# Where the operands of TensorE begin in a 64-byte line of SBUF

## The chip, the cores and the metric

One core of one Trainium2 chip (trn2). The time is the device time of one execution in microseconds (us), the median of several runs. The kernel before takes 1748.18 us, the median of three runs from 1745.37 to 1749.04.

## The reference

The input is 256 tokens of width 1024, in float32. Two blocks follow each other.

The first block is a token mixer and a layer of experts. The mixer projects the normed input to gates, a short causal convolution and an mLSTM of 8 heads; its two branches are projected, gated and added, and projected once more. The experts are PEER: 8 heads pick 16 of 16384 experts for each token, and `out = gelu(h @ u) * gate @ v` is taken over the picked ones.

The second block has two layers, one with latent attention (MLA), one with attention over q, k and v (MoBA, which at this length is plain attention with a bias by distance). Each is followed by a layer norm, a convolved and gated feed-forward network (FFN) with 22 chunks of 128 hidden columns, and a layer norm.

```
h  = modulate(rms_norm(x))           # per block and layer
y  = h @ W                           # q, k, v, gates, branches, u, v, FFN in and out
```

Nearly all work is matrix products of the 256 tokens with weights of 1024 rows or columns.

## The kernel before, in words

Activations lie transposed: 128 partitions, 8 chunks (`KC`) of the model width, 256 tokens (`T`). Weights come from HBM as slabs of 128 x 1024 float32 values, 512 KB each, into `wraw`. To keep float32 precision every operand is split into a high part (`hi`, of type float32r, made by a copy on ScalarE, ACT) and a low part (the rest, made by a subtraction on VectorE, DVE). A product is then three matmuls: high by high, high by low, low by high. `mm3` (L398 to L403) issues them: with weights as the stationary operand, loaded anew for each matmul, and the activations as the moving operand of 256 columns: whi with the activation's high part (L401), whi with its low part (L402), wlo with its high part (L403). `block` does this for the 8 chunks of a slab, 24 matmuls; `half` (L473 to L475) does the same for the output projections of the attentions.

In three projections to values (`vform`, L448 to L450: w_v, ml_uv, mo_v) and in the expert output (`row`, L1276 to L1278, 128 slabs of v) the roles are turned: the activation is stationary, and the slab's high and low parts, whi and wlo, are the moving operands, 512 columns at a time.

The order of the work is written out by hand. `use` takes the next slab of a plan, starts the load of a later one on SP's queue (5 slabs ahead) and splits the next ones (`warm`, L312 and L320, three buffers each for whi and wlo, `buffer` gives them). Small generators that evacuate PSUM and do the element-wise work are advanced before and after each block. While the chip does this, loads of the modulation matrices (`mraw`, L519) run at a rate set for each stage (`RATES`).

The pairs of activations are named after their stage: h (mixer input), ya, ym, mx (mixer), h2 (expert input), hh and hl (inputs of the second block's layers; the mixer's h bears the names hh and hl in the trace as well), o (attention output), lat (latent), gb (FFN hidden), pre (before a layer norm).

A pool gives its tiles one after the other, at multiples of 32 bytes. `off_line` (L590) asks for a tile of 32 bytes and leaves it unused, so that what follows begins half a line of 64 bytes further on. By the sizes in the code and the addresses that the compiled program gives its tiles, all pairs but two begin 32 bytes into such a line, high and low part alike: h, ya, ym, mx, h2, hh, lat, both o, and gb of layer 0. The first exception is gb of layer 1, where `4 * l` words are left out at the front (L1803): its high part begins 16 bytes in and its low part 48. The second is pre, whose rows are 258 words long, so that each chunk begins 8 bytes further on. The slabs whi and wlo begin at 0, and so do ah and al, the stationary operands of the expert output.

Of the kernel before, what the change touches and what calls it, by code (L numbers as in the profile page):

```python
# [11 lines left out]
F32 = mybir.dt.float32  # L12
F32R = mybir.dt.float32r
# [8 lines left out]
P = 128  # L22
T = 256
D = 1024
KC = 8
# [20 lines left out]
ROW_UNITS = 8  # L46
PAUSES = [3, 2, 2, 2, 2, 2, 2, 1, 0, 3, 3]
NFF = 22
EPS = 1e-6
LN_EPS = 1e-5  # L50
TINY = 1e-30
# [213 lines left out]
class Body:  # L265
# [64 lines left out]
    def buffer(self, n, pool, part, name):  # L330
        if n in self.spare:
            return self.spare[n][part]
        if self.extra and n >= self.n_extra and (n - self.n_extra) % 5 < 2:
            pool = self.extra[part]
        return pool.tile([P, D], F32R, name=name)

    def load(self, n):
        if self.plan is None:
# [248 lines left out]
        nc.gpsimd.tensor_tensor(r[:, :width], v[:, :width], self.mhalf[:, :width], ALU.pow)  # L587
        return r

    def off_line(self, pool, name):  # L590

        pool.tile([P, 8], F32, name="half" + name)

    def pool_l(self, name, bufs=1):
        return self.tc.tile_pool(name=name, bufs=bufs, reuse_waits="tile")
# [117 lines left out]
    def mixer(self):  # L713
        nc, a = self.nc, self.a
        with ExitStack() as ctx:
            self.tmps = ctx.enter_context(self.pool_l("tmps1", 14))
            sp = ctx.enter_context(self.pool_l("mix", 1))
            self.mctx = ExitStack()
            mp = self.mctx.enter_context(self.pool_r("mraw", 4))
            rp = ctx.enter_context(self.pool_l("mixr", 2))  # L720
            act8 = lambda n, tag=None: (sp.tile([P, KC, T], F32R, name=n + "h", tag=(tag or n) + "h"),
                                         sp.tile([P, KC, T], F32R, name=n + "l", tag=(tag or n) + "l"))
            f8 = lambda n, tag=None: sp.tile([P, KC, T], F32, name=n, tag=tag or n)
            x = self.x

# [4 lines left out]
            v = {}  # L730
# [12 lines left out]
            for w in LOADS:  # L743
                n = int(w[1])
# [14 lines left out]
            st = self.pst()  # L759
            xn = f8("xn", "qk")  # L760
            a1 = self.cp.tile([P, KC], F32, name="a1")
            self.off_line(sp, "h")
            h = act8("h")
            ws, lows, pts = [], {}, {}
            pair = [sp.tile([P, 2, D], F32R, name="w3" + m, tag="ya" + m) for m in "hl"]
            for n in range(3, START_SLABS):
                self.spare[n] = [t[:, n - 3] for t in pair]

# [49 lines left out]
            for w in START:  # L818
                if w in left:
                    n = left.index(w) + 1  # L820
# [144 lines left out]
            ya = act8("ya")  # L965
# [26 lines left out]
            for j in range(8):  # L992
                gc, gx, gb = g_cxb(j)
# [2 lines left out]
                self.block("w_x", j, h, gx)  # L996
                self.block("w_b", j, h, gb)

            self.off_line(sp, "ym")
            ym = act8("ym")  # L1000

            def g_fin():
# [108 lines left out]
    def peer(self):  # L1111
        tc, nc, a = self.tc, self.nc, self.a
        NB = 88
        with ExitStack() as ctx:
            self.tmps = ctx.enter_context(self.pool_l("tmps2", 4))
            sp = ctx.enter_context(self.pool_l("pe", 1))
# [2 lines left out]
            iT.append(sp.tile([P, T // 2], F32, name="nT"))  # L1119
            hctx = ExitStack()  # L1120
            hp = hctx.enter_context(self.pool_l("peh", 1))
            self.off_line(hp, "h2")
            h = (hp.tile([P, KC, T], F32R, name="h2h"), hp.tile([P, KC, T], F32R, name="h2l"))
            r = self.rstd(self.st2, 2, EPS, D)
            self.rows.step(PAUSES[9])
            bc = self.bcast2(r)
# [29 lines left out]
            zb = gp = None  # L1156
# [71 lines left out]
            for i2 in range(P):  # L1228
                if i2 == N0:
                    for _ in self.side or ():  # L1230
                        pass
                    self.side = None
                    tctx.close()
                    zp = zctx.enter_context(self.pool_r("zb", 1))
                    zb = zp.tile([P, P - NB, T], F32, name="zb")
                    self.off_line(zp, "zb")
                    gctx = ExitStack()
                    gp = gctx.enter_context(self.pool_l("oneh", 2))
                if i2 >= N0 and ng < 64:
                    self.spawn(g_group(ng))  # L1240
                    ng += 1
                if i2 == N0 + 67:
                    gctx.close()
                    vp2 = zctx.enter_context(self.pool_r("pv2", 2))
                    asplit(0)
                self.block("u", i2, h, g_z(i2))
# [41 lines left out]
            for i2 in range(P - 1):  # L1288
                w = self.use(("v", i2, 0, D))
# [21 lines left out]
            w = self.use(("v", P - 1, 0, D))  # L1311
# [5 lines left out]
            part = lambda tt, hf: yt[:, (2 * tt + hf) * 512:(2 * tt + hf + 1) * 512]  # L1317
# [35 lines left out]
            self.xctx = ExitStack()  # L1353
            xp = self.xctx.enter_context(self.pool_r("xp2"))
            x2 = xp.tile([P, KC, T], F32, name="x2")
            h = self.h = (xp.tile([P, KC, T], F32R, name="hh"), xp.tile([P, KC, T], F32R, name="hl"))
            crow = xp.tile([P, D], F32, name="crow")
            nc.sync.dma_start(crow, self.crow)
            self.crow = crow
            self.rt = xp.tile([P, 3, T], F32, name="rt")  # L1360
            nc.sync.dma_start(self.rt, rt[:, 0:3])
            ht = za[:, 16:24]
            piece = lambda j: tr[j // 2][:, (j % 2) * T:(j % 2 + 1) * T]
# [224 lines left out]
    def ln_cols(self, idx, nxt, pre=None):  # L1588
        nc = self.nc
        g, b = self.colr("ln_g", 8 * idx, 8), self.colr("ln_b", 8 * idx, 8)  # L1590
        AB = ag = None
        self.pre = pre
        if nxt is not None:
            s, c = nxt
            AB = self.cp.tile([P, KC, 2], F32, name=f"lnAB{idx}")
            for n, w in enumerate((g, b)):
                nc.vector.scalar_tensor_tensor(AB[:, :, n], c, 1.0, w, op0=ALU.add, op1=ALU.mult)
            nc.vector.tensor_tensor(AB[:, :, 1], AB[:, :, 1], s, ALU.add)
            self.split(AB, pre[0][:, :, T:], pre[1][:, :, T:])
            ag = self.cp.tile([P, 16], F32, name=f"lnag{idx}")  # L1600
            nc.vector.tensor_scalar_mul(ag[:, 0:8], g, ALPHA)
            nc.vector.tensor_scalar_mul(ag[:, 8:16], b, ALPHA)
        self.lnc = g, b, AB, ag
        self.lnb, self.lnbs = {}, (self.lnbuf[:, :T], self.lnbuf[:, T:])
# [191 lines left out]
    def ffn(self, l, act, ctx, pts, prate=0.0):  # L1796

        nc = self.nc
        sp = ctx.enter_context(self.pool_l(f"ffn{l}", 1))
        if l == 0:  # L1800
            self.off_line(sp, "gb")

        gh, gl = (sp.tile([P, NFF * T + 4 * l], F32R, name="gb" + n)[:, 4 * l:].rearrange("p (a t) -> p a t", t=T) for n in "hl")  # L1803

        def g_ab(j):
            ge = {}

            def ga(pt):
                ac = self.tmp("fa")
                taps = [self.col("fconv", (3 * l + t) * NFF + j) for t in range(3)]  # L1810
                nc.scalar.activation(ac, pt[:, :T], AF.Identity, bias=self.col("fconvb", l * NFF + j), scale=taps[2])
                yield "post"
                for t in (1, 0):
                    s = 2 - t
                    nc.vector.scalar_tensor_tensor(ac[:, s:T], pt[:, 0:T - s], taps[t], ac[:, s:T], op0=ALU.mult, op1=ALU.add)
                nc.scalar.activation(ac, ac, AF.Gelu_apprx_tanh)
                ge[0] = ac

            def gb(pt):
                if j < NFF - 1:  # L1820
                    yield "post"
                y = self.tmp("fy")
                nc.vector.tensor_tensor(y, pt[:, :T], ge[0], ALU.mult)
                nc.scalar.activation(gh[:, j], y, AF.Copy)
                yield "post"
                self.lo_of(y, gh[:, j], gl[:, j])
            return ga, gb
        gens = [g for j in range(NFF) for g in g_ab(j)]
        names = self.ffn_names(l)
        for g, pt in zip(gens, pts):  # L1830
            self.spawn(self.g_lead(g)(pt))
        self.blocks(names[3:6], act, gens[3:6])
        for k in range(6, len(names)):
            if k == 12:
                self.prate = prate
            self.block(*names[k], act, gens[k])
        return gh, gl

    def second(self):
        nc = self.nc  # L1840
        with ExitStack() as ctx:
            self.tmps = ctx.enter_context(self.pool_l("tmps3", 12))
            sp = ctx.enter_context(self.pool_l("s2", 1))
            self.mpool = ctx.enter_context(self.pool_l("mraw3", 2))
            self.prs = ctx.enter_context(self.pool_l("pairs", 3))
            act8 = lambda pool, n: (pool.tile([P, KC, T], F32R, name=n + "h"), pool.tile([P, KC, T], F32R, name=n + "l"))
            self.z = sp.tile([P, KC, T], F32, name="z")
            h = self.h
            hx = ctx.enter_context(self.pool_l("whi2", 2)), ctx.enter_context(self.pool_l("wlo2", 2))
# [24 lines left out]
            mctx = ExitStack()  # L1874
            sp = mctx.enter_context(self.pool_l("mla", 1))
            self.rp = mctx.enter_context(self.pool_l("mlar", 3))
            self.off_line(sp, "o")
            o = act8(sp, "o")
            lat = sp.tile([P, 4, T], F32, name="lat")
            la = (sp.tile([P, 4, T], F32R, name="lath"), sp.tile([P, 4, T], F32R, name="latl"))  # L1880
            sts = {}

            def g_lat(b):
# [105 lines left out]
            gb = self.ffn(0, h, fctx, pts, RATES[2])  # L1989
# [10 lines left out]
            mctx = ExitStack()  # L2000
            sp = mctx.enter_context(self.pool_l("moba", 1))
            self.rp = mctx.enter_context(self.pool_l("mobar", 3))
            self.off_line(sp, "o")
            o = act8(sp, "o")
            vs = sp.tile([P, 2, D], F32, name="vs")
            qn, kn = qk_of(sp)

# [37 lines left out]
            gb = self.ffn(1, h, fctx, pts, RATES[5])  # L2045
# [32 lines left out]
```

## Time and profile before

| | |
|---|---|
| Median of three runs | 1748.18 us |
| The profiled execution's own time | 1751.12 us |
| Its span, first to last instruction | 1749.4 us |
| PE (TensorE matmul) busy | 1716.4 us, 98% |
| DVE (VectorE) busy | 1383.5 us, 79% |
| ACT (ScalarE) busy | 1040.0 us, 59% |
| DMA engines, mean rate | 212 GB/s |
| Granted TensorE clock, mean | 0.992 |

The busy time of PE is the union of its matmuls, which overlap one another: a matmul is recorded from the start of its reading to the modelled end of its writing. How fast PE goes is seen in the distance between the starts of two neighbours, and that is had from the number of matmuls in a stretch. [...]

### The profile page before, as it was taken

The page shows a single profiled execution, that of the slowest core. Times are in us where ns is not written, and L with a number is a line of the kernel's source. Part 1 is how long each engine was busy: PE and PEld are TensorE (multiplying, and loading weights), DVE is VectorE, ACT ScalarE, POOL GpSimd, SP SyncE. Part 2 cuts the span into 40 slices and gives each one's busy share as a digit, 9 for nine tenths or more (in the row PEclk, how much of TensorE's full clock was granted, in tenths as well). Part 3 has the DMA queues.
Part 4 walks back from the last instruction along what each step waited for, and adds up shares of the span by engine and source line. Part 5 has one row for each costly group of instructions (what it writes and reads, how often), then busy time and mean ns, then how long its engine had stood idle before and what let it go on. Part 6 is the DMA issues. An engine that isn't in the chain of part 4 may idle for free.

```text
span 1749.4 us, 33343 instructions
## 1 busy us (share of the span) xinstructions
PE 1716.4 (98%) x12720; PEld 1598.1 (91%) x12720; DVE 1383.5 (79%) x2845; ACT 1040.0 (59%) x1910; POOL 198.4 (11%) x235
## 2 busy tenths in 40 slices
PE   8999999999999999999999999989999999999997
PEld 4899999799999999998888888888999998999997
DVE  3788778589988889997888888876799778688754
ACT  3764444455554999985555554555676547567542
POOL 1110000000010654540000000030200000020001
PEclk8999999999999999999999999999999999999998
DMA  7676677555555544447898888852467674446552
GB/s 271 247 263 215 229 253 242 193 170 171 192 181 181 169 157 158 157 159 251 299 326 300 288 299 306 286 199 97 129 229 277 249 250 163 149 130 207 188 180 77
DMA packets 102400, 371.17 MB, mean 212 GB/s; under 512 B 11456, under 2 KB 11968, under 8 KB 101856
## 3 DMA queue, kind: packets, MB, share of 16 engines
q1 hardware_dynamic: 101664, 365.76, 61.6%
q0 software_dynamic: 576, 3.29, 0.5%
q8 instruction: 99, 1.62, 0.4%
q14 instruction: 61, 0.50, 0.1%
HBM read 365.99 MB, written 2.10 MB: 210 GB/s over the span
## 4 chain that ended last, share of the span: by engine, by line
PE 90%; DVE 4%; ACT 3%; issue 1%; DMA 1%; POOL 1%; POOLq 0%; ACTq 0%; DVEq 0%; SPq 0%
PE ps L401 19%; PE ps L403 19%; PE ps L402 19%; PE ps L1277 6%; PE ps L1278 6%; PE ps L1276 6%; PE ps L1205 2%; PE ps L568 1%; PE ps L448 1%; PE ps L449 1%; PE ps L450 1%; PE ps L473 1%; PE ps L739 1%; PE ps L475 1%; PE ps L474 1%
## 5 line engine op out<-in xcount | busy, mean ns | idle before, releaser
L312 ACT ACTIVATE whi<-wraw 128x1024 fp32r<-128x1024 f32 (+1 forms) x548 | 574.2, 1050 | 446.9 <-PE ps L402 195.5
L320 DVE TENSOR_TENSOR wlo<-wraw,whi 128x1024 fp32r<-128x1024 f32 (+1 forms) x538 | 649.7, 1212 | 51.7 <-ACT whi L312 50.5
L401 PE MATMUL ps<-hh,whi 128*128 128x256 f32 x1240 | 352.9, 285 | 1.9 <-ACT hh L675 1.5
L403 PE MATMUL ps<-hh,wlo 128*128 128x256 f32 x1240 | 348.5, 281 | 4.5 <-DVE wlo L320 4.5
L402 PE MATMUL ps<-hl,whi 128*128 128x256 f32 x1240 | 348.1, 281 | 1.5 <-DVE hl L397 1.3
L401 PE MATMUL ps<-h2h,whi 128*128 128x256 f32 x1152 | 329.9, 286 | 0.0
L403 PE MATMUL ps<-h2h,wlo 128*128 128x256 f32 x1152 | 322.3, 280 | 0.2 <-DVE wlo L320 0.2
L402 PE MATMUL ps<-h2l,whi 128*128 128x256 f32 x1152 | 321.3, 279 | 0.0
L401 PEld LDWEIGHTS ps<-hh,whi 128*128 128x128 f32 x1240 | 234.1, 189 | 5.4 <-ACT hh L675 2.6
L403 PEld LDWEIGHTS ps<-hh,wlo 128*128 128x128 f32 x1240 | 233.9, 189 | 5.4 <-DVE wlo L320 5.4
L402 PEld LDWEIGHTS ps<-hl,whi 128*128 128x128 f32 x1240 | 234.0, 189 | 3.1 <-DVE hl L397 2.8
L403 PEld LDWEIGHTS ps<-h2h,wlo 128*128 128x128 f32 x1152 | 216.4, 188 | 0.6 <-DVE wlo L320 0.6
L401 PEld LDWEIGHTS ps<-h2h,whi 128*128 128x128 f32 x1152 | 216.5, 188 | 0.4 <-ACT za L673 0.4
L402 PEld LDWEIGHTS ps<-h2l,whi 128*128 128x128 f32 x1152 | 216.9, 188 | 0.0
L1277 PE MATMUL ps<-whi,al 128*128 128x512 f32 x512 | 199.5, 390 | 0.8 <-DVE al L397 0.8
L1278 PE MATMUL ps<-wlo,ah 128*128 128x512 f32 x512 | 199.2, 389 | 0.0
L1276 PE MATMUL ps<-whi,ah 128*128 128x512 f32 x512 | 199.2, 389 | 0.0
L519 DVE SCALAR_TENSOR_TENSOR mraw<-mraw,crow 128x1024 f32<-128x1024 f32 x128 | 157.0, 1227 | 0.0
L1197 POOL TENSOR_SCALAR L<-iota,i1T,eT 128x128 bf16<-128x128 f32 x128 | 123.2, 970 | 295.9 <-DVE mT L1498 139.1
L1277 PEld LDWEIGHTS ps<-whi,al 128*128 128x128 f32 x512 | 96.1, 188 | 22.1 <-DVE al L397 1.9
L1276 PEld LDWEIGHTS ps<-whi,ah 128*128 128x128 f32 x512 | 96.1, 188 | 19.9
L1278 PEld LDWEIGHTS ps<-wlo,ah 128*128 128x128 f32 x512 | 96.1, 188 | 19.8
(449 smaller groups left out, 2971.8 us busy)
## 6 DMA issues: line engine op xcount, KB each, us to landing
wraw<-u SPq DMA_DIRECT2D x128, 512.0 KB, 3.3
wraw<-v SPq DMA_DIRECT2D x128, 512.0 KB, 5.4
mraw<-mod SPq DMA_DIRECT2D x88, 512.0 KB, 3.9
wraw<-fa SPq DMA_DIRECT2D x44, 512.0 KB, 4.1
wraw<-fb SPq DMA_DIRECT2D x44, 512.0 KB, 4.3
mraw<-w_ada SPq DMA_DIRECT2D x40, 512.0 KB, 4.2
wraw<-fo SPq DMA_DIRECT2D x32, 512.0 KB, 4.5
wraw<-wq SPq DMA_DIRECT2D x16, 512.0 KB, 4.3
```

Source lines behind the costliest of these rows:

```text
L312: nc.scalar.activation(t[:, :hi - lo], self.raws[self.n_hi][:, :hi - lo], AF.Copy)
L320: e.tensor_tensor(t[:, :n], self.raws[self.n_lo][:, :n], self.his[self.n_lo].bitcast(F32)[:, :n], ALU.subtract)
L401: mm(out, lh, rh, start=start, stop=False, **kw)
L402: mm(out, lh, rl, start=False, stop=False, **kw)
L403: mm(out, ll, rh, start=False, stop=stop, **kw)
L448: mm(pts[tt][hf], ah, wh[:, s], start=kc == 0, stop=False)
L519: nc.vector.scalar_tensor_tensor(raw, raw, 1.0, self.crow, op0=ALU.mult, op1=ALU.mult, accum_out=acc)
L1197: nc.gpsimd.tensor_scalar(L[:, k], iota, i1, e, op0=ALU.is_equal, op1=ALU.mult)
L1205: nc.tensor.matmul(pg[:, k * P:(k + 1) * P], L[:, k], half[:, k, h], start=h == 1, stop=h == 0)
L1276: mm(o, ah, w[0][:, s], start=first, stop=False)
L1277: mm(o, al, w[0][:, s], start=False, stop=False)
L1278: mm(o, ah, w[1][:, s], start=False, stop=last)
```

## The change

A table `AT` gives each pair two places in a line, in words of 4 bytes, for the high and the low part. `acts` asks for a tile that is one line (16 words) longer than needed and takes the part of it that begins at that place. The pads of `off_line` in front of the pairs go; one pad of 32 bytes is kept or put where the tiles before or after would otherwise lie off a line (`half_line`, in front of ym, behind zb and behind rt). whi and wlo become one line longer too, and a slab that will be moving (`MOVING`: w_v, v, ml_uv, mo_v) begins 16 bytes in (whi) or 48 (wlo), unless it falls on the two extra buffers of the second block, which stay at 0; a slab that will be stationary begins at 0 as before. Two small constants of each layer norm, `lnAB` and `lnag`, move from the pool `cp` to a pool of the second block, 384 bytes in all, as much as whi and wlo gain.

The starts, in bytes into a 64-byte line, high part / low part:

| pair | before | after |
|---|---|---|
| h (mixer) | 32 / 32 | 16 / 16 |
| ya | 32 / 32 | 4 / 4 |
| ym | 32 / 32 | 60 / 60 |
| mx | 32 / 32 | 48 / 48 |
| h2 (experts) | 32 / 32 | 16 / 48 |
| hh (second block) | 32 / 32 | 16 / 48 |
| lat | 32 / 32 | 8 / 8 |
| o, first and second attention | 32 / 32 | 48 / 16 and 0 / 32 |
| gb, layer 0 | 32 / 32 | 4 / 4 |
| gb, layer 1 | 16 / 48 | 8 / 56 |
| whi / wlo as moving operands | 0 / 0 | 16 / 48 |

```diff
+LINE = 16
+AT = dict(h=(4, 4), ya=(1, 1), ym=(15, 15), mx=(12, 12), h2=(4, 12), hh=(4, 12), la=(2, 2), o0=(12, 4), o1=(0, 8), gb0=(1, 1),
+          gb1=(2, 14), w=(4, 12))
+MOVING = ("w_v", "v", "ml_uv", "mo_v")
...
         if self.extra and n >= self.n_extra and (n - self.n_extra) % 5 < 2:
-            pool = self.extra[part]
-        return pool.tile([P, D], F32R, name=name)
+            return self.extra[part].tile([P, D], F32R, name=name)
+        at = AT["w"][part] if self.plan[n][0] in MOVING else 0
+        return pool.tile([P, D + LINE], F32R, name=name)[:, at:at + D]
...
-    def off_line(self, pool, name):
-
-        pool.tile([P, 8], F32, name="half" + name)
+    def acts(self, pool, name, kc=KC, tag=None):
+
+        return tuple(pool.tile([P, kc * T + LINE], F32R, name=name + m, tag=(tag or name) + m)[:, at:at + kc * T]
+                     .rearrange("p (a t) -> p a t", t=T) for m, at in zip("hl", AT[name]))
+
+    def half_line(self, pool, name):
+
+        pool.tile([P, LINE // 2], F32, name="half" + name)
...
-            self.off_line(hp, "h2")
-            h = (hp.tile([P, KC, T], F32R, name="h2h"), hp.tile([P, KC, T], F32R, name="h2l"))
+            h = self.acts(hp, "h2")
...
-            h = self.h = (xp.tile([P, KC, T], F32R, name="hh"), xp.tile([P, KC, T], F32R, name="hl"))
+            h = self.h = self.acts(xp, "hh")
...
+            self.half_line(xp, "rt")
...
-            AB = self.cp.tile([P, KC, 2], F32, name=f"lnAB{idx}")
+            AB = self.np.tile([P, KC, 2], F32, name=f"lnAB{idx}")
...
-        gh, gl = (sp.tile([P, NFF * T + 4 * l], F32R, name="gb" + n)[:, 4 * l:].rearrange("p (a t) -> p a t", t=T) for n in "hl")
+        gh, gl = self.acts(sp, f"gb{l}", NFF)
...
```

## Rows read from the trace of the kernel before

**Rows 1.** The page: PE's busy time and instructions; the granted clock in 40 slices.
```profile
PE 1716.4 (98%) x12720; PEld 1598.1 (91%) x12720; DVE 1383.5 (79%) x2845; ACT 1040.0 (59%) x1910; POOL 198.4 (11%) x235
...
PEclk8999999999999999999999999999999999999998
```

**Rows 2.** The page: the chain that ended last, by engine and line.
```profile
PE 90%; DVE 4%; ACT 3%; issue 1%; DMA 1%; POOL 1%; POOLq 0%; ACTq 0%; DVEq 0%; SPq 0%
PE ps L401 19%; PE ps L403 19%; PE ps L402 19%; PE ps L1277 6%; PE ps L1278 6%; PE ps L1276 6%; PE ps L1205 2%; PE ps L568 1%; PE ps L448 1%; PE ps L449 1%; PE ps L450 1%; PE ps L473 1%; PE ps L739 1%; PE ps L475 1%; PE ps L474 1%
```

**Rows 3.** Stretches: A:B, length, each engine's busy time (count), clock, DMA share, GB/s.
```profile
78.50:90.00 11.50, 11.50 (x51) 9.27 (x50) 11.26 (x21) 6.09 (x10) 0.02 (x1) 1.00 0.97 367
102.00:116.00 14.00, 14.00 (x123) 14.00 (x122) 10.54 (x16) 8.25 (x14) 0.00 (x0) 1.00 0.94 348
...
398.00:488.00 90.00, 90.00 (x767) 90.00 (x766) 85.63 (x281) 47.07 (x69) 0.00 (x0) 1.00 0.57 187
500.00:558.00 58.00, 58.00 (x500) 58.00 (x499) 54.95 (x145) 30.87 (x45) 3.60 (x3) 1.00 0.58 187
830.00:1120.00 290.00, 290.00 (x1281) 239.99 (x1280) 242.66 (x410) 151.95 (x225) 1.68 (x3) 1.00 0.87 302
1300.00:1370.00 70.00, 70.00 (x597) 70.00 (x596) 65.62 (x115) 43.63 (x67) 0.00 (x0) 1.00 0.80 282
1373.60:1435.60 62.00, 62.00 (x529) 62.00 (x528) 47.38 (x75) 30.44 (x41) 0.00 (x0) 1.00 0.70 249
1600.00:1670.00 70.00, 70.00 (x602) 70.00 (x601) 51.39 (x76) 42.63 (x66) 0.00 (x0) 1.00 0.59 189
1675.90:1736.50 60.60, 60.60 (x526) 60.60 (x526) 31.08 (x42) 22.31 (x28) 0.00 (x0) 1.00 0.41 127
```

**Rows 4.** Lines 402, 474 and 1276: count, duration (min/median/max), first and last start.
```profile
L402 PE MATMUL ps<-hl,whi x1240: 276/278/416, 37.9 to 1675.6; 128*128 128x256 f32 x177, 128*40 128x256 f32 x1
L402 PE MATMUL ps<-h2l,whi x1152: 276/278/282, 342.2 to 791.1; 128*128 128x256 f32 x192
L402 PE MATMUL ps<-gbl,whi x352: 275/276/278, 1373.7 to 1736.6; 128*128 128x256 f32 x176
...
L402 PE MATMUL ps<-yal,whi x64: 277/280/282, 251.6 to 275.3; 128*128 128x256 f32 x64
L402 PE MATMUL ps<-yml,whi x64: 276/281/288, 275.6 to 298.1; 128*128 128x256 f32 x64
L402 PE MATMUL ps<-mxl,whi x64: 277/279/385, 298.5 to 321.5; 128*128 128x256 f32 x64
L402 PE MATMUL ps<-latl,whi x48: 277/280/282, 1169.0 to 1197.6; 128*128 128x256 f32 x48
...
L474 PE MATMUL ps<-ol,whi x128: 277/280/281, 1210.5 to 1541.4; 128*128 128x256 f32 x128
...
L1276 PE MATMUL ps<-whi,ah x512: 388/389/398, 791.4 to 1140.5; 128*128 128x512 f32 x171
```

**Rows 5.** Tile gbh: ScalarE's writes in the FFN of layer 0 and of layer 1.
```profile
L1824 ACT ACTIVATE gbh<-t_fy x15: 400/419/422, 1293.6 to 1368.7; 128x256 fp32r<-128x256 f32 x15
...
L1824 ACT ACTIVATE gbh<-t_fy x16: 400/400/420, 1590.2 to 1671.1; 128x256 fp32r<-128x256 f32 x16
```

**Rows 6.** Line 1205, the one-hot matmuls of the experts: count, durations, first and last start.
```profile
L1205 PE MATMUL ps<-R,L x512: 218/219/233, 570.7 to 782.8; 128*128 128x128 f16 x171
```

**Rows 7.** Waits in the expert output: who waited for whom, us, times, longest.
```profile
ACT whi L312 <- DMA wraw<-v: 4.2, 2, 2.2
...
PE ps L1277 <- DVE al L397: 0.8, 2, 0.7
```

More of the change, by code (lines that the diff above doesn't have):

```diff
@@ L720, in mixer @@
             rp = ctx.enter_context(self.pool_l("mixr", 2))
-            act8 = lambda n, tag=None: (sp.tile([P, KC, T], F32R, name=n + "h", tag=(tag or n) + "h"),
-                                         sp.tile([P, KC, T], F32R, name=n + "l", tag=(tag or n) + "l"))
+            act8 = lambda n, tag=None: self.acts(sp, n, tag=tag)
             f8 = lambda n, tag=None: sp.tile([P, KC, T], F32, name=n, tag=tag or n)
@@ L761, in mixer @@
             a1 = self.cp.tile([P, KC], F32, name="a1")
-            self.off_line(sp, "h")
             h = act8("h")
             ws, lows, pts = [], {}, {}
-            pair = [sp.tile([P, 2, D], F32R, name="w3" + m, tag="ya" + m) for m in "hl"]
+            pair = [sp.tile([P, 2 * D + LINE], F32R, name="w3" + m, tag="ya" + m)[:, :2 * D].rearrange("p (a t) -> p a t", t=D) for m in "hl"]
             for n in range(3, START_SLABS):
@@ L997, in mixer @@
                 self.block("w_b", j, h, gb)
-            self.off_line(sp, "ym")
+            self.half_line(sp, "ym")
             ym = act8("ym")
@@ L1235, in peer @@
                     zb = zp.tile([P, P - NB, T], F32, name="zb")
-                    self.off_line(zp, "zb")
+                    self.half_line(zp, "zb")
                     gctx = ExitStack()
@@ L1599, in ln_cols @@
             self.split(AB, pre[0][:, :, T:], pre[1][:, :, T:])
-            ag = self.cp.tile([P, 16], F32, name=f"lnag{idx}")
+            ag = self.np.tile([P, 16], F32, name=f"lnag{idx}")
             nc.vector.tensor_scalar_mul(ag[:, 0:8], g, ALPHA)
@@ L1799, in ffn @@
         sp = ctx.enter_context(self.pool_l(f"ffn{l}", 1))
-        if l == 0:
-            self.off_line(sp, "gb")
-        gh, gl = (sp.tile([P, NFF * T + 4 * l], F32R, name="gb" + n)[:, 4 * l:].rearrange("p (a t) -> p a t", t=T) for n in "hl")
+        gh, gl = self.acts(sp, f"gb{l}", NFF)
         def g_ab(j):
@@ L1843, in second @@
             sp = ctx.enter_context(self.pool_l("s2", 1))
+            self.np = ctx.enter_context(self.pool_l("lnc", 1))
             self.mpool = ctx.enter_context(self.pool_l("mraw3", 2))
             self.prs = ctx.enter_context(self.pool_l("pairs", 3))
-            act8 = lambda pool, n: (pool.tile([P, KC, T], F32R, name=n + "h"), pool.tile([P, KC, T], F32R, name=n + "l"))
             self.z = sp.tile([P, KC, T], F32, name="z")
@@ L1876, in second @@
             self.rp = mctx.enter_context(self.pool_l("mlar", 3))
-            self.off_line(sp, "o")
-            o = act8(sp, "o")
+            o = self.acts(sp, "o0")
             lat = sp.tile([P, 4, T], F32, name="lat")
-            la = (sp.tile([P, 4, T], F32R, name="lath"), sp.tile([P, 4, T], F32R, name="latl"))
+            la = self.acts(sp, "la", 4)
             sts = {}
@@ L2002, in second @@
             self.rp = mctx.enter_context(self.pool_l("mobar", 3))
-            self.off_line(sp, "o")
-            o = act8(sp, "o")
+            o = self.acts(sp, "o1")
             vs = sp.tile([P, 2, D], F32, name="vs")
```

## The prediction

> **What bounds the kernel now.** [...] The view to read is the table of stretches. A stretch in which PE is busy throughout and does one kind of matmul gives the distance: its length plus one duration (0.28 us for 256 columns, 0.39 for 512), divided by the count, since the count includes what overlaps its start.
>
> That gives, in ns per matmul [rows 3]:
> - 256 columns, high and low parts both 32 bytes into a line: 90.28/767 = 117.7 and 58.28/500 = 116.6 (h2), 70.28/597 = 117.7 and 70.28/602 = 116.7 (hh, the two FFN layers), 62.28/529 = 117.7 (gb, layer 0), 14.28/123 = 116.1 (h of the mixer; one matmul more or less there is 1 ns).
> - 256 columns, high part 16 bytes in and low part 48 (gb of layer 1, the one pair that has such starts already): 60.88/526 = 115.7.
> - 512 columns, moving slab at 0: 290.39/1281 = 226.7 with the stationary side at 0 too (expert output), 11.89/51 = 233.2 with the stationary side 32 bytes in (`vform`).
>
> The clock is 1.00 in all these stretches, so it explains none of the differences. The two rows of gb do the same work on the same buffers, layer for layer; only the starts differ, and layer 1 is 2.0 ns a matmul ahead of layer 0. That is the evidence for a gain. The evidence against reading it too surely is in the same table: with nothing but 32/32 the distance is 116.6 in one stretch and 117.7 in the next, in the very same loop. A part of what separates two rows is thus not the start.
>
> **The change part by part.** No instruction, transfer or wait is added or removed; the parts are the starts of the operands, pair by pair. I price a matmul at 16/48 at 115.7, and the state of today at the mean of the rows for that tile.
>
> 1. h2, 32/32 to 16/48: 1152 groups of three [rows 4] = 3456 matmuls. Today (767 x 117.7 + 500 x 116.6)/1267 = 117.3; 1.6 ns less, 3456 x 1.6 = 5.5 us. Bounds: 0.9 ns (today all at 116.6) gives 3.1, 2.0 ns gives 6.9.
> 2. hh, 32/32 to 16/48: of the 1240 groups that stand under the names hl and whi [rows 4], 440 are the mixer's h (57 blocks of 8, less 16 groups that run from a spare buffer); 800 remain, 2400 matmuls. Today the mean of 117.7 and 116.7, 1.5 ns more than 115.7: 3.6 us, bounds 2.4 and 4.8.
> 3. o of the first attention, 32/32 to 48/16: half of 128 groups, 192 matmuls [rows 4]: 0.3 us.
> 4. The value slabs, 0 to 16 (whi) and 48 (wlo), with 512 columns: 1536 matmuls in the expert output [rows 4], and some 200 in the three `vform` calls. No row shows a 512-column read from such a start. The nearest row on one side is gb's step, about 1.5 ns a matmul whatever its length: 2.3 us saved. The nearest on the other is the step between the two 512-column rows, 233.2 − 226.7 = 6.5 ns for an operand that leaves the line's start: 1536 x 6.5 = 10.0 us lost. The same step taken as a gain is the far bound of the third rival. I take 2.3 us saved, as gb's row is of the very starts that these slabs get.
> 5. h of the mixer, 32/32 to 16/16: 456 groups, 1368 matmuls. Equal starts other than 32 stand in no steady row; between nothing and 116.6 − 115.7 = 0.9 ns: I take 0.7, 1.0 us.
> 6. ya (4/4), ym (60/60), mx (48/48), lat (8/8), o of the second attention (0/32), gb layer 0 (4/4) and layer 1 (8/56): 64 x 3 + 48 + 64 + 352 = 656 groups [rows 4], 1968 matmuls, whose new starts no row shows. gb's step of 2.0 ns either way bounds them: 3.9 us won or lost. I take nothing; layer 1 gives up the best row there is, layer 0 leaves the worst.
> 7. Side effects. ScalarE's write of gb takes 400 to 419 ns at 32 and 400 at 16, so starts off 32 don't slow the writers [rows 5]; were they slower by 19 ns a piece, ACT and DVE have room in all stretches of [rows 3] (the fullest long one is DVE's in h2, 85.63 of 90 us). The one-hot tiles of line 1205 lose their 32 bytes with h2's pad: 512 matmuls [rows 6], with the 6.5 ns step 3.3 us either way; I take nothing. `lnAB` and `lnag` move to another pool and are written by the same instructions, on DVE and beside PE's matmuls: nothing.
>
> Sum: 5.5 + 3.6 + 0.3 + 2.3 + 1.0 = 12.7 us. All of it lies on PE, which sets the end. What could be late next: a slab's period in h2 falls by 1.4%, so DVE goes from 95% to 96.5% of it; in the mixer the DMA engines are at 0.94 of their time and up to 0.97 in its `vform`, so the 1.0 us of part 5 is the least sure; in the expert output the DMA engines go from 0.87 to 0.88 of their time [rows 3], and a transfer has ended ScalarE's wait there for 4.2 us in all, DVE has held PE for 0.8 [rows 7]. Neither takes back more than 1 us. The profiled execution took 1751.1 us (span 1749.4 and 1.7 around it), so it would take 1738.4; it lies 2.9 us over the median of the runs, and from that median, 1748.2, the sum gives 1735.5.
>
> [...]
>
> **The rivals.**
> - The 512-column slabs lose (slower). [...] For it: 233.2 against 226.7, for leaving the start on one side only. Against it: there it is the stationary side, and gb's step shows that places inside the line differ. Price 10.0 us: 1758. It decides where the distance in the expert output passes 226.7 and the 12.7 − 2.3 = 10.4 us of the other parts are not won either. Chance 9%.
> - The start doesn't matter, the rows show two or three rhythms into which the same stream falls. For it: 116.6 and 117.7 with the same starts. Against it: 115.7 is seen only with 16/48, over a whole layer. Then the starts at 16 and 48 change nothing, and those that are no multiple of 16 (4, 8, 56 and 60: ya, ym, lat and both gb, 64 x 2 + 48 + 352 = 528 groups, 1584 matmuls) may cost gb's 2.0 ns, 3.2 us: 1748 to 1751. Chance 13%. [...]
> - All parts reach their good end: 6.9 + 4.8 + 0.4 + 10.0 + 1.2 + 3.9 = 27.2 us, 1721; half the way there from the forecast is 1728. Chance of more than 20 us saved: 15%.
> - The change doesn't do what it says: if a pool begins 32 bytes off from what the sizes in the code give, 16/48 becomes 48/16 and 4 becomes 36. Chance 3%; the time would lie anywhere between 1735 and 1752.
>
> **How the numbers follow.** The forecast, 4 to 20 us saved (1728 to 1744), has 60%; the rest is above. Its time is 1735.5. The 80% range leaves out the upper half of the first two rivals and the far end of the third: 1722 to 1749. A change of under 0.2%, 3.5 us, can't be told from none here. Faster by that: 60 + 15 + 2 of the last rival's 3, 77%; the same: 12%, most of the second rival and the last one's third; slower: 11%, the first rival and the end of the second.
>
> **What would show it.** In the profile after: 115.7 in the stretches of h2 and hh; below 226.7 in the expert output; the same counts of instructions. Wrong steps show as 116.6 to 117.7 in h2 and hh (second rival), or as 228 and more in the expert output (first rival). A new PE wait for DVE in h2 or for a slab's transfer in the expert output would show that the gain was won and given back.

## The result, and the profile after

The changed kernel takes 1764.3 us (median of 4 runs, 1762.97 to 1765.61), the kernel before beside it 1746.78 us (4 runs, 1743.95 to 1749.04). The ratio is 1.0101, 95% interval 1.0082 to 1.0121: slower by 1%, where 1735.5 us was forecast and 1749 was the end of the range. The profiled execution took 1763.19 us with a span of 1761.4. The two medians lie 17.5 us apart, the two profiled executions 12.0: that of before was the slowest of its four runs. The traces account for the 12.0; what makes up the rest is not shown.

What the page shows is a kernel that does the same work: PE's 12720 matmuls, and the counts and busy times of DVE and ACT (1384.0 and 1040.2 us), are those of before, the times to within 0.5 us [rows 1].

```profile
PE 1728.5 (98%) x12720; PEld 1607.2 (91%) x12720; DVE 1384.0 (79%) x2845; ACT 1040.2 (59%) x1910; POOL 196.0 (11%) x235
...
PEclk9999999999999999999999999999999999999998
```

PE waits, all told, hardly longer than it did: the rows of its waits come to 23.9 us before and 24.3 after. From the page of before, then from that of after, two of the costliest groups; last on the line is the idle time just before, and what ended it (before had 0.8 us at the last of them [rows 7]):

```profile
L403 PE MATMUL ps<-h2h,wlo 128*128 128x256 f32 x1152 | 322.3, 280 | 0.2 <-DVE wlo L320 0.2
```
```profile
L409 PE MATMUL ps<-h2h,wlo 128*128 128x256 f32 x1152 | 323.7, 281 | 1.9 <-DVE wlo L325 1.9
...
L1285 PE MATMUL ps<-whi,al 128*128 128x512 f32 x512 | 202.1, 395 | 0.6 <-DVE al L403 0.5
```

One wait for wlo in h2 has grown from 0.2 to 1.9 us; it is 0.2 to 1.3 in the kernels below. But for that, the 12.0 us by which the two spans differ lie in the time from one matmul's start to the next one's. The stretches of [rows 3], in the profile after (the short ones at the front are left out: the stages lie elsewhere in time):

```profile
398.00:488.00 90.00, 90.00 (x761) 90.00 (x760) 85.52 (x281) 46.27 (x68) 0.00 (x0) 1.00 0.56 182
500.00:558.00 58.00, 58.00 (x491) 58.00 (x490) 54.53 (x143) 30.38 (x47) 5.16 (x4) 1.00 0.57 187
830.00:1120.00 290.00, 290.00 (x1259) 236.35 (x1258) 238.96 (x404) 148.95 (x220) 1.68 (x3) 1.00 0.85 297
1300.00:1370.00 70.00, 70.00 (x597) 70.00 (x596) 67.33 (x116) 45.79 (x71) 0.00 (x0) 1.00 0.83 293
...
1600.00:1670.00 70.00, 70.00 (x597) 70.00 (x596) 53.95 (x80) 45.33 (x72) 0.00 (x0) 1.00 0.63 202
```

The clock is 1.00 throughout. Counted as in the prediction, (length + one duration)/count: h2 118.6 and 118.7 ns a matmul (before 117.7 and 116.6), the expert output 230.7 (226.7), hh 117.7 and 117.7 (117.7 and 116.7). Where 115.7 was forecast, no stretch shown is below 117.7.

A second reading needs no stretch. Line 408 (402 before) issues one matmul of each group of three, and its rows give the first and the last start of a stage:

```profile
L408 PE MATMUL ps<-h2l,whi x1152: 275/281/288, 341.2 to 794.3; 128*128 128x256 f32 x192
...
L408 PE MATMUL ps<-gb0l,whi x176: 277/283/290, 1381.6 to 1445.0; 128*128 128x256 f32 x176
L408 PE MATMUL ps<-gb1l,whi x176: 280/283/288, 1685.3 to 1748.5; 128*128 128x256 f32 x176
...
L408 PE MATMUL ps<-yal,whi x64: 277/285/290, 249.9 to 274.3; 128*128 128x256 f32 x64
L408 PE MATMUL ps<-yml,whi x64: 276/278/283, 274.7 to 296.9; 128*128 128x256 f32 x64
...
L408 PE MATMUL ps<-lal,whi x48: 278/283/287, 1177.8 to 1206.9; 128*128 128x256 f32 x48
...
L1284 PE MATMUL ps<-whi,ah x512: 388/392/397, 794.5 to 1149.2; 128*128 128x512 f32 x171
```

Against [rows 4], stage by stage, in us:

| stage | before | after | differs |
|---|---|---|---|
| up to h2's first start | 342.2 | 341.2 | −1.0 |
| h2, first to last start | 448.9 | 453.1 | +4.2 |
| expert output, first to last start | 349.1 | 354.7 | +5.6 |
| from there to the end of the span | 608.9 | 612.2 | +3.3 |

With −0.1 between the second and the third this is the 12.0. The first row hides a loss: the first matmul of the mixer's h starts 3.0 us earlier in the profile after (34.9 against 37.9 us), and the stage from there to h2 takes 2.0 longer. In the last row, gb of layer 0 takes 63.4 us instead of 61.8 and gb of layer 1 63.2 instead of 60.6 (before: 175 groups of three at the 117.7 and 115.7 of [rows 3] are 61.8 and 60.7). A group of three is the best unit for what follows: (last − first)/(count − 1). For the expert output it goes from 349.1/511 = 683.2 to 354.7/511 = 694.1 ns; the 226.7 and 230.7 of the stretches, times three, are 680.1 and 692.1, without the few groups that wait.

### The profile page after: what moved, and what is told of

Read it like the earlier page. It is cut to its first block, busy times and chain, and to the rows that moved or that the text cites. A ratio compares the mean times of both kernels' runs of the same rounds, so it can differ in the third digit from the quotient of the medians.

```text
span 1761.4 us, 33342 instructions
## 1 busy us (share of the span) xinstructions
PE 1728.5 (98%) x12720; PEld 1607.2 (91%) x12720; DVE 1384.0 (79%) x2845; ACT 1040.2 (59%) x1910; POOL 196.0 (11%) x235
## 4 chain that ended last, share of the span: by engine, by line
PE 71%; DVE 4%; ACT 2%; issue 1%; POOL 0%; DMA 0%; POOLq 0%; ACTq 0%; DVEq 0%
PE ps L407 15%; PE ps L408 15%; PE ps L409 15%; PE ps L1285 6%; PE ps L1284 5%; PE ps L1286 5%; PE ps L1213 2%; DVE wlo L325 1%; PE ps L479 1%; PE ps L480 1%; PE ps L481 1%; DVE mraw L525 1%; PE ps L574 1%; PE ps L454 1%; PE ps L456 1%
## 5 line engine op out<-in xcount | busy, mean ns | idle before, releaser
L409 PE MATMUL ps<-hhh,wlo 128*128 128x256 f32 x800 | 224.4, 280 | 4.1 <-DVE wlo L325 4.1
L407 PE MATMUL ps<-hhh,whi 128*128 128x256 f32 x800 | 227.1, 284 | 0.8 <-ACT hhh L686 0.8
L408 PE MATMUL ps<-hhl,whi 128*128 128x256 f32 x800 | 225.7, 282 | 1.2 <-DVE hhl L403 1.1
L409 PEld LDWEIGHTS ps<-hhh,wlo 128*128 128x128 f32 x800 | 150.8, 188 | 4.7 <-DVE wlo L325 4.7
L408 PEld LDWEIGHTS ps<-hhl,whi 128*128 128x128 f32 x800 | 151.1, 189 | 2.7 <-DVE hhl L403 2.4
L407 PEld LDWEIGHTS ps<-hhh,whi 128*128 128x128 f32 x800 | 151.3, 189 | 2.0 <-ACT hhh L686 1.6
L407 PE MATMUL ps<-hh,whi 128*128 128x256 f32 (+1 forms) x440 | 126.0, 286 | 0.7 <-ACT hh L686 0.7
L408 PE MATMUL ps<-hl,whi 128*128 128x256 f32 (+1 forms) x440 | 123.6, 281 | 0.2 <-DVE hl L403 0.2
L409 PE MATMUL ps<-hh,wlo 128*128 128x256 f32 (+1 forms) x440 | 123.4, 280 | 0.3 <-DVE wlo L325 0.3
```

The source lines that it names most:

```text
L407: mm(out, lh, rh, start=start, stop=False, **kw)
L408: mm(out, lh, rl, start=False, stop=False, **kw)
L409: mm(out, ll, rh, start=False, stop=stop, **kw)
```

## The experiments

The places of operands below are taken from the addresses in the compiled programs. "Distance" is from here on the place of the moving operand minus that of the stationary one, modulo 256 bytes. The line of 64 bytes is only a unit for naming starts; no run shows that the memory has such lines. Two first theories stand in the first expectation, A and B; C came after its miss. Each row shown is the line that issues the second matmul of a group (for the expert output the first, `ps<-whi,ah`).

**The pairs alone.** The changed kernel with the slabs as they were before, 1024 words long and at 0:

```
-        at = AT["w"][part] if self.plan[n][0] in MOVING else 0
-        return pool.tile([P, D + LINE], F32R, name=name)[:, at:at + D]
+        return pool.tile([P, D], F32R, name=name)
```

> The pairs of activations at the new starts, the slabs whi and wlo 1024 words long and at 0 as before. Theory A (spacing of the buffers): with a line more each, the three whi and three wlo buffers lie alternately in the first and the second half of 128 bytes, and the matmuls of a group lose where whi and wlo are not in the same half. Then h2 falls from 118.4 ns a matmul (355.2 a group of three) to 116.4 (349.2), the second block's hh from 117.8 to 116.4, the expert output from 230.5 back to 226.7; total 1764.3 - 6.9 - 3.4 - 5.5 - 2 = 1746 to 1748. Theory B (the starts themselves are the cost): h2 and hh stay at 118, only the expert output comes back; 1758. Both: gb, ya and lat (starts 4 and 8) stay at 120 to 121.

Measured: 1762.28 us, ratio to before 1.0072 (1.0049 to 1.0096).

```profile
L407 PE MATMUL ps<-h2l,whi x1152: 275/281/284, 342.1 to 788.0; 128*128 128x256 f32 x192
...
L1283 PE MATMUL ps<-whi,ah x512: 390/393/404, 788.3 to 1145.7; 128*128 128x512 f32 x171
```

h2 takes 445.9 us, 3.0 less than before: the gain forecast for it is there in part. But the expert output, whose slabs and stationary tiles have their old starts in a line, is slower than in either kernel: 357.4 us, 699.4 ns a group. Neither theory had that. What is left of the change in that stage is that `lnAB` and `lnag`, 384 bytes, have left a pool that lies ahead of the slabs: whi and wlo lie 384 bytes lower, while ah and al, in a pool on the other side of the memory, stay. Theory C is that this distance decides.

**The slabs alone.** The kernel before with the slabs' part of the change and the constants' move; the pairs as before. Then the same with all slabs at 0, so that they are only a line longer:

```
+        at = AT["w"][part] if self.plan[n][0] in MOVING else 0
+        return pool.tile([P, D + LINE], F32R, name=name)[:, at:at + D]
...
-AT = dict(w=(4, 12))
+AT = dict(w=(0, 0))
```

> The kernel before with the slab part alone: whi and wlo one line longer, moving ones at 16 and 48; all pairs as before. Theory A: h2 rises from 117.5 to some 118.5 to 119, hh and the mixer too, the expert output is at 230 as in the changed kernel; 1757 to 1760. Theory B: the pairs stay at 117.1 to 117.5, only the expert output loses 5.5 us: 1752.

> The kernel before with whi and wlo one line longer, but every slab at 0: the spacing of the buffers alone. Theory A: h2 and hh rise as in the kernel with the slab part alone; the expert output loses a part of its 3.8 ns a matmul too; 1752 to 1757. Theory B: nothing changes, 1747.

Measured: 1760.11 us, ratio 1.0074 (1.0045 to 1.0102), and 1760.2 us, ratio 1.0072 (1.0047 to 1.0097). First the one, then the other:

```profile
L407 PE MATMUL ps<-h2l,whi x1152: 277/280/285, 341.6 to 793.8; 128*128 128x256 f32 x192
...
L1281 PE MATMUL ps<-whi,ah x512: 387/392/400, 794.1 to 1148.7; 128*128 128x512 f32 x171
```
```profile
L407 PE MATMUL ps<-h2l,whi x1152: 277/280/285, 341.8 to 793.2; 128*128 128x256 f32 x192
...
L1281 PE MATMUL ps<-whi,ah x512: 388/393/398, 793.4 to 1148.2; 128*128 128x512 f32 x171
```

452.2 and 451.4 us in h2, 354.6 and 354.8 in the expert output. Moving the slabs to 16 and 48 makes no difference to the stage as a whole. What both kernels share does: the slabs are 64 bytes longer, so that neighbouring buffers no longer have the same place modulo 256, and the constants have moved. Sorted by the buffer that a slab fell on, h2's groups without a wait take 353.3, 353.7 and 357.5 ns in the first kernel (352.4 before, on all three), and the expert output 690.2, 688.8 and 696.0 (680.3). In the second kernel the same three buffers take 696.0, 688.2 and 689.2 in the expert output, with whi at distances of 128, 0 and 192 instead of 144, 16 and 208. So 16 bytes more or less are worth up to 7 ns a group, either way, and cancel over the three.

**All pairs at 16/48**, slabs as before, the constants still moved:

```
...
+AT = {n: (4, 12) for n in "h ya ym mx h2 hh la o0 o1 gb0 gb1".split()}
...
-        at = AT["w"][part] if self.plan[n][0] in MOVING else 0
-        return pool.tile([P, D + LINE], F32R, name=name)[:, at:at + D]
+        return pool.tile([P, D], F32R, name=name)
```

> Slabs as before, every pair at 16 / 48 (h, ya, ym, mx, lat, both o, both gb as well as h2 and hh). Theory A: all 256-column groups near 116.4 or 115.7 a matmul; 1738 to 1741, the best of the four, and against the kernel with the new starts and the old slabs gb, ya and lat gain 5 ns a matmul, 6 us in all. Theory B: all 256-column groups at 118; 1755.

Measured: 1758.52 us, ratio 1.0063 (1.0038 to 1.0088).

```profile
L406 PE MATMUL ps<-gb0l,whi x176: 279/286/286, 1374.8 to 1437.3; 128*128 128x256 f32 x176
L406 PE MATMUL ps<-gb1l,whi x176: 279/286/286, 1678.2 to 1740.8; 128*128 128x256 f32 x176
...
L1282 PE MATMUL ps<-whi,ah x512: 390/393/404, 784.4 to 1141.8; 128*128 128x512 f32 x171
```

Both gb now have the very starts that I had taken for the gain, and take 357 and 358 ns a group, more than with 32/32 before (353). The second block's slabs fall on two sets of buffers, which with the constants moved lie 128 bytes apart modulo 256; sorted by them, groups of the same layer take 360.0 ns (104 groups) and 353.1 (71), in both layers. The expert output is at 699.4 again.

**The constants alone.** The kernel before; nothing is changed but the pool of `lnAB` and `lnag`:

```
-            AB = self.cp.tile([P, KC, 2], F32, name=f"lnAB{idx}")
+            AB = self.np.tile([P, KC, 2], F32, name=f"lnAB{idx}")
...
-            ag = self.cp.tile([P, 16], F32, name=f"lnag{idx}")
+            ag = self.np.tile([P, 16], F32, name=f"lnag{idx}")
...
+            self.np = ctx.enter_context(self.pool_l("lnc", 1))
```

> The kernel before with one thing changed: lnAB and lnag move from cp to a pool of the second block. No start in a 64-byte line changes; all tiles of the left pools lie 384 bytes lower, those of the right pools (ah, al, the second block's hh) stay. Theory C (a matmul's pace goes by the distance, modulo 256 bytes, between its moving operand and the stationary operand beside it): the distance in the expert output goes from 0 to 128, so 226.8 ns a matmul become 232.5 as in the first and the fourth kernel, 8.8 us; h2 (both sides move together) stays at 117.5; total 1755 to 1758. Theory B (only the start in the 64-byte line counts) and theory A (only which half of 128 bytes whi and wlo lie in): no change, 1747.

Measured: 1758.82 us, ratio 1.0057 (1.0044 to 1.007), as theory C expected. The expert output takes 357.3 us:

```profile
L1276 PE MATMUL ps<-whi,ah x512: 389/393/405, 788.8 to 1146.1; 128*128 128x512 f32 x171
```

**Its converse.** The kernel before with only ah and al 128 bytes further on modulo 256, the slabs where they were:

```
-                ah = vp2.tile([P, T], F32R, name="ah")
-                al = vp2.tile([P, T], F32R, name="al")
+                ah = vp2.tile([P, T + 64], F32R, name="ah")[:, 32:32 + T]
+                al = vp2.tile([P, T + 64], F32R, name="al")[:, 32:32 + T]
```

> The kernel before with only ah and al, the stationary operands of the expert output, 128 bytes further on; the slabs whi and wlo and all pairs stay at their places. It is the converse of e5_constants_moved, which moved the slabs and left ah and al. Theory C (what counts is the distance of the moving from the stationary operand, modulo 256 bytes): the expert output goes from 680.3 to 697 ns for a group of three, 512 x 17 = 8.7 us: 1755 to 1758; all other stages as before. Theory of absolute places (a slab is read faster from one half of 256 bytes than from the other, wherever the stationary operand lies): nothing changes, 1747 to 1749.

Measured: 1757.93 us, ratio 1.005 (1.0032 to 1.0067).

```profile
L1276 PE MATMUL ps<-whi,ah x512: 390/393/404, 789.5 to 1146.8; 128*128 128x512 f32 x171
```

Two different operands were moved, and both times the stage takes 357.3 us, 699.2 ns a group instead of 683.2. So it is the distance and not the place of either. The sizes are steady: the stage takes 349.1 to 349.4 us in the four kernels with the distance 0 (before and three of the kernels below), 357.3 or 357.4 in the four with 128. Nor does it hang on what ACT does at the same time: here the groups without a wait during which ACT is busy for less than a fifth take 697.2 ns (237 groups), those with more than four fifths 697.1 (258). ah and al have two buffers each, so a run holds several distances modulo 1024: in the kernel before, groups without a wait take 680.0 and 680.5 ns at 256 and 768; here they take 697.1 to 697.3 in all four combinations of 128, 384, 640 and 896. This is why I count modulo 256, though 0 and 512 stand in none of these kernels for a whole group.

**One distance for all.** The kernel before with every pair at 16/48 past the place of whi and wlo modulo 256 (pads in front of the pairs), slabs and constants untouched; then the same with every pair 128 bytes further on; then the first with ah and al 16 bytes lower:

```
+PAD = dict(h=0, ya=192, ym=32, mx=0, h2=0, hh=224, o0=0, la=192, o1=0, gb0=0, gb1=0)
...
+    def acts(self, pool, name, kc=KC, tag=None):
+
+        return tuple(pool.tile([P, kc * T + 8], F32R, name=name + m, tag=(tag or name) + m)[:, 4:4 + kc * T]
+                     .rearrange("p (a t) -> p a t", t=T) for m in "hl")
...
-PAD = dict(h=0, ya=192, ym=32, mx=0, h2=0, hh=224, o0=0, la=192, o1=0, gb0=0, gb1=0)
+PAD = dict(h=128, ya=192, ym=32, mx=0, h2=128, hh=96, o0=128, la=192, o1=128, gb0=128, gb1=128)
...
-                ah = vp2.tile([P, T], F32R, name="ah")
+                ah = vp2.tile([P, T + 64], F32R, name="ah")[:, 60:60 + T]
```

> Slabs and constants as before; every pair of activations at 16 / 48 in its line and, by pads, 16 and 48 bytes past the places of whi and wlo modulo 256, which is the distance that gb of layer 1 has in the kernel before. Theory C: all groups of 256 columns at 346.7 to 348 a group of three (115.6 to 116 a matmul), the expert output at 226.8; against before 1152 x 5 + 1256 x 4 + 176 x 6 ns = 12 us less, 1735 to 1738. Theory B: 355 to 356 a group as in the changed kernel for most pairs: 1755.

> The same kernel with every pair of activations 128 bytes further on: the same places in the 64-byte line and in 128 bytes, the other distance modulo 256. Theory C: groups of 256 columns at 352 to 355, the expert output unchanged; 1750 to 1758, 15 to 20 us over the kernel without the 128. Theory B and theory A: no difference between the two.

> The kernel with one distance for all pairs, and in the expert output ah and al 16 bytes below the place of whi and wlo modulo 256, so that the slabs stay where they are and still lie 16 past the stationary side. Theory C as far as 256 columns show it (a distance of 16 beats 32 and others): below 226.8 ns a matmul, down to 224 (4 us). If a stationary operand off its line costs what the slab at 16 did (688.7 a group): 229.6, 4 us more. Groups of 256 columns as without it.

Measured: 1742.18 us, ratio to before 0.9965 (0.9952 to 0.9977); 1749.77 us, ratio 1.001 (0.9996 to 1.0024); 1744.03 us, ratio 0.9974 (0.9961 to 0.9987). The first is faster than both kernels. The rows of the three, in that order:

```profile
L403 PE MATMUL ps<-h2l,whi x1152: 275/275/282, 343.2 to 788.4; 128*128 128x256 f32 x192
...
L403 PE MATMUL ps<-gb0l,whi x176: 275/275/275, 1367.7 to 1428.3; 128*128 128x256 f32 x176
L403 PE MATMUL ps<-gb1l,whi x176: 278/280/282, 1669.8 to 1731.6; 128*128 128x256 f32 x176
```
```profile
L403 PE MATMUL ps<-h2l,whi x1152: 277/281/288, 342.7 to 790.2; 128*128 128x256 f32 x192
...
L403 PE MATMUL ps<-gb0l,whi x176: 279/282/288, 1373.4 to 1435.5; 128*128 128x256 f32 x176
L403 PE MATMUL ps<-gb1l,whi x176: 277/280/282, 1675.3 to 1736.0; 128*128 128x256 f32 x176
```
```profile
L403 PE MATMUL ps<-gb0l,whi x176: 278/280/283, 1363.6 to 1425.4; 128*128 128x256 f32 x176
L403 PE MATMUL ps<-gb1l,whi x176: 274/275/276, 1663.6 to 1724.2; 128*128 128x256 f32 x176
...
L1287 PE MATMUL ps<-whi,ah x512: 387/390/401, 781.0 to 1131.7; 128*128 128x512 f32 x171
```

The gain was less than expected from the first, and the loss from the second was 7.6 us instead of 15 to 20: sizes that I missed. A reason for a part of it shows in gb. In the first kernel layer 0 and layer 1 have the same addresses for both operands, and take 60.6 and 61.8 us, 346 and 353 ns a group. In the third, with these same addresses again, it is the other way round: 61.8 and 60.6. So there are two rhythms into which one stream falls, and the placement doesn't choose between them. At the other distance, in the second kernel, both occur too: 62.1 and 60.7 us, so gb there tells nothing of the 128 bytes. h2 has the same addresses in the first, the third and the next experiment's kernel, and takes 445.2, 443.5 and 442.6 us. Each kernel has one trace here; whether the rhythm changes from one execution to the next is not shown. The third kernel's own question is small: 16 bytes on ah and al make 350.7 us of 349.1, 3.1 ns a group, between the two values expected.

**Starts that are no multiple of 16.** The first of these three with five pairs moved by some bytes. Either such a start costs, or only the distance from the weights counts, which changes here by no more than 8 to 12 bytes:

```
+AT = dict(ya=(1, 1), ym=(7, 7), la=(1, 1), gb0=(1, 1), gb1=(2, 6))
```

> The kernel e6_one_distance with only the starts of five pairs moved by a few bytes, to places that are no multiple of 16: ya, latent and gb of layer 0 at 4 / 36 (from 16 / 48), gb of layer 1 at 8 / 56, ym at 28 / 60. Everything else, and each tile's place, stays. [...] If 60 is a place of its own, as ym at 60/60 showed in the changed kernel (352.7), ym stays near 350 here. [...]

Measured: 1749.16 us, ratio 1.0002 (0.9988 to 1.0016), against 0.9965 for the kernel it was made from.

```profile
L404 PE MATMUL ps<-gb0l,whi x176: 279/282/288, 1359.8 to 1423.4; 128*128 128x256 f32 x176
L404 PE MATMUL ps<-gb1l,whi x176: 277/282/285, 1664.9 to 1727.8; 128*128 128x256 f32 x176
...
L404 PE MATMUL ps<-yal,whi x64: 279/284/288, 246.5 to 270.9; 128*128 128x256 f32 x64
L404 PE MATMUL ps<-yml,whi x64: 277/278/278, 271.2 to 293.5; 128*128 128x256 f32 x64
```

gb of layer 0 (4/36) takes 63.6 us, 363 ns a group, ya 363 in groups without other work between, gb of layer 1 (8/56) 62.9 us, 359 ns; ym at 28/60 takes 354, less than in the kernel before (22.5 us for 63 groups, 357) and 3 more than in the kernel that this one is made from (351). A start 4 or 8 bytes past a multiple of 16 costs 6 to 17 ns a group, one 12 past it costs nothing that stands out of the two rhythms. Such starts are slow at other distances too: from the experiment with the pairs alone (4/4) to the one with all pairs at 16/48, gb of layer 0 goes from 364.6 to 360.1 ns on one set of buffers and from 360.5 to 353.1 on the other. But the distance leaves the multiples of 16 together with the start, since the weights lie at 0; which of the two costs is not separated.

## Why the prediction was wrong

The step that failed is the first sentence of the second part: that "the parts are the starts of the operands, pair by pair". The change moves more than starts in a line. It takes 384 bytes out of a pool ahead of the slabs and makes each slab 64 bytes longer, and by that the operands of one matmul change their distance modulo 256 bytes. I had put the move of `lnAB` and `lnag` down as nothing, because I looked only at who writes them. Alone it costs 16 ns for each of 512 groups, 8.2 us (357.3 − 349.1), and a ratio of 1.0057. In the changed kernel the longer slabs spread the buffers over several distances, and the stage loses 5.6 instead.

By the terms of the sum (12.7 us saved were forecast, 12.0 lost were traced):

- Value slabs: forecast 2.3 saved, traced 5.6 lost. The first rival had the right stage and a price (10.0) of the right order, but its reason, that leaving a line's start costs, fell: the slabs cost as much when they begin at 0 and are only longer, with the constants moved. Its point of decision, 226.7, was passed with 230.7. The 6.5 ns from which its price came were read as the stationary operand's start; in `vform` the distance is another too (224 instead of 0), and no run tells the two apart there.
- h2: forecast 5.5 saved, traced 4.2 lost, 1.7 of them the longer wait for wlo. A gain was there but was outweighed, and the starts alone don't explain it. In the five kernels with slabs of equal places and h2's high part at a distance of 16 the stage takes 442.6 to 445.9 us, with 144 and the same starts it takes 447.5; with 32/32 448.1 to 449.7 (before, 448.9, and two others): up to 6.3 us saved against before, 1.4 where the distance is 144. With longer slabs it takes 451.4 to 453.1, with either start.
- hh, o and the rest of the second block without gb: forecast 3.9 saved; traced 3.3 lost with gb's 4.2 and latent's 0.4, which leaves 1.3 saved. In hh itself no gain: 117.7 and 116.7 in the two layers became 117.7 and 117.7.
- ya, latent and gb, taken as nothing with bounds of 3.9 us: gb lost 4.2, ya 0.7, latent 0.4, together 5.3. Mis-sized: the bound was gb's 2.0 ns, and a start at 4 or 8 costs up to 5.5 ns a matmul (16.6/3 between the experiments with starts at 16/48 and at 4/36). That a start off a multiple of 16 may cost gb's 2.0 ns (6.0 a group), from which the second rival has its 3.2 us, was shown by no run before; 4 and 8 past one then came with 6 to 17 ns a group, 12 past with 3.
- h of the mixer: forecast 1.0 saved; 213.4 us from its first to its last start became 214.6.
- The evidence itself, 117.7 against 115.7 for gb, was one draw of a rhythm: of the six gb stages with a high part at 16 and a distance of 16 throughout, three take 346.7 ns a group and three 353.3, as much as 32/32 takes in the kernel before. The second rival named it and had 13%; I argued against it that 115.7 stood "only with 16/48, over a whole layer". A whole layer is one sample of the rhythm, not 526 of them. In the converse experiment gb of layer 1 has the very place that it has in the kernel before, and its group takes 353.3 ns instead of 346.7:

```profile
L402 PE MATMUL ps<-gbl,whi x176: 278/280/282, 1681.3 to 1743.1; 128*128 128x256 f32 x176
```

That side effects on other engines are nothing held, but for the 1.7 us in h2: the busy times of DVE and ACT are as before. That more was lost in the medians (17.5 us) than in the traces (12.0) stays open. What the experiments don't settle: which stationary operand meets the moving one, that of the same matmul or the next one's, which is loaded meanwhile (in the kernel before, at 700.06 us a matmul recorded as 0.28 us long and the next one's weight load of 0.19 us start together); what chooses a rhythm; and why 12 past a multiple of 16 costs nothing that stands out (354 ns a group against 351). Why the distance counts is not shown, and I have no rule that gives the times of the single buffers with longer slabs.

## What to carry to other kernels

Where TensorE is busy throughout, as here for 98% of the span, a change of a tile's size or pool moves every tile behind it: list the addresses of both operands of each hot matmul before and after, and compare their distances, not only the starts. Here 128 bytes of distance were worth 16 ns in 683 in the expert output. A difference between two stretches is evidence for a cause only if the same placement gives the same number elsewhere in the trace or in another program; a long stretch is still a single sample: with one placement, gb's 176 groups took 346 ns each in one layer and 353 in the other. Starts 4 or 8 bytes past a multiple of 16 came with 6 to 17 ns a group here and with no gain. Try a layout first by the one stage that it touches.

## What the runs showed that was not expected

- A distance of 0 modulo 256 bytes between a 512-column moving operand and the stationary one gives 680 ns for a group of three, 16 gives 683.4, 128 gives 697. Moving either operand alone by 128 bytes costs the same 17 ns of 680.
- Two rhythms of one stream: in one, every one of 175 groups of gb takes 345 to 348 ns; in the other they swing from 347 to 358, with a mean of 353.3. At the distance 16 the recorded durations tell them apart too: a median of 275 in the one, of 280 in the other (at 144, the fast one has 280 as well). With 32/32, layer 0 of the kernel before has neither: each of its groups takes 353 or 354.
